# The up projection of two MLPs by seven block products in place of eight, in step with the down projection of the pair before

## The chip, the core and the metric

The kernel runs on one core of a Trainium2 chip. TensorE (PE) multiplies, VectorE (DVE) and ScalarE (ACT) prepare operands and take results out of PSUM, GpSimd (POOL) does little, and SyncE (SP) issues the loads from HBM. The metric is the device time of one execution in microseconds, the median of the runs.

## The reference

A hybrid decoder trunk of two layers over 256 tokens of width 2048, all in float32: a latent attention mixer (MLA), then a Mamba-2 mixer (SSM), each followed by a dense MLP with a squared relu. The MLPs are what the change is about:

```
for i in range(DEPTH):                       # DEPTH = 2
    h = rms_norm(x, mix_norm_g[i])
    mix = mla_mixer(h, ...) if i == 0 else ssm_mixer(h, ...)
    x = x + mix
    h = rms_norm(x, mlp_norm_g[i])
    x = x + squared_relu_mlp(h, mlp_w_in[i], mlp_w_out[i])

def squared_relu_mlp(h, w_in, w_out):        # (256, 2048), (2048, 8192), (8192, 2048)
    u = jax.nn.relu(h @ w_in)
    return (u * u) @ w_out
```

## The kernel before

**Three matmuls for one product.** TensorE is fed with a rounded float32 form. So each float32 operand is split into a high part h (the rounded value) and a low part lo (what is left), and a product is ah*wh + ah*wl + al*wh: the three `matmul` calls of `block` (lines 227 to 229). The stationary operand is a 128x128 tile of the activations, transposed (features on partitions, tokens in columns); the moving operand is a 128x512 tile of the weights. Results gather in a PSUM bank of 128 tokens by 512 columns.

**Weights.** `Flow` (line 59) holds a list of all weight pieces in the order of their use. A piece is 512 rows by 512 columns, 1 MB, laid out as 128 partitions by 4 k-tiles by 512 columns. `load` (line 70) issues its transfer on SP's queue into one of three `raw` buffers. `convert` (line 81) makes h and lo for half a piece at a time (two k-tiles, 1024 columns): a copy on ACT (line 101) into one of three `wh` buffers, then a subtraction on DVE (line 102) into one of three `wl` buffers. `piece` (line 106) hands out the halves; before it hands out one it has asked for loads three pieces on and conversions two halves on (`ahead`, (3, 2)).

**The MLP** (line 371). The hidden width of 8192 is cut into 16 blocks of 512 columns, taken four at a time, as a chunk. For each block the up projection runs over 16 k-tiles and two token tiles, 96 matmuls of 4 pieces, into two banks of the pool `acc` (4 banks). ACT takes each bank out with relu, scaled by the row's normalisation (line 384), and squares it (line 385). One step later four TensorE transposes (line 210) bring it into `yp` or `sm` (2 banks each), and `split_out` (lines 203, 204) makes h and lo of it in `k4` tiles. Behind the four blocks of a chunk comes their down projection: four column blocks of the output, each over the chunk's 16 k-tiles, 96 matmuls into two banks, which DVE adds to the residual x (line 307). In the last chunk `finalize` (line 275) also prepares the next layer's input, or the result is stored (line 398).

**What sets the order.** TensorE executes in the order in which the source issues. The other engines' and queues' orders are set when the kernel is built, by a scheduler that places an instruction where it expects its inputs and a free buffer; each engine then keeps to its order. `later(n, fn)` (line 153) puts small work, such as transposes, off by n further steps; `tick` (line 156) ends a step. Weight conversion, taking out of PSUM and residual additions share the queues of DVE and ACT.

The MLA and SSM stages use the same `block` and `Flow`. `boundary_begin` and `finalize` leave the next stage's input as four pairs of tiles (h and lo), each of 4 k-tiles by 256 tokens.

Of the kernel before, what the change touches and what calls it, by code (L numbers as in the profile page):

```python
# [20 lines left out]
F32 = mybir.dt.float32  # L21
F32R = mybir.dt.float32r
# [35 lines left out]

class Flow:


    def __init__(self, nc, pools, seq, ahead):
        self.nc, self.pools, self.seq, self.ahead = nc, pools, seq, ahead
        self.raw, self.loaded, self.used, self.done = {}, 0, 0, 0
        self.halves, self.split = [], {}
        for i, (_, _, nk, n) in enumerate(seq):
            step = nk if nk * n <= 1024 else nk // 2
            self.halves += [(i, k, step, n) for k in range(0, nk, step)]

    def load(self, upto, split=None, beside=None):  # L70
        while self.loaded < min(upto, len(self.seq)):
            _, src, nk, n = self.seq[self.loaded]
            t = self.pools["raw"].tile([P, 2048], F32, tag="raw", name=f"wr{self.loaded}")
            for o, z in split or ((0, nk * n),):
                self.nc.sync.dma_start(t[:, o:z], src[:, o:z])
                if split:
                    beside()
            self.raw[self.loaded] = t
            self.loaded += 1

    def convert(self, upto):
        while self.done < min(upto, len(self.halves)):
            j = self.done
            i, k, nk, n = self.halves[j]
            self.load(i + 1)
            raw = self.raw[i][:, k * n:(k + nk) * n]
            h = self.pools["wh"].tile([P, 1024], F32R, tag="wh", name=f"wh{j}")
            lo = self.pools["wl"].tile([P, 1024], F32R, tag="wl", name=f"wl{j}")
            if n == 64:
                for q, t in enumerate((h, lo)):  # L90
                    v = t.rearrange("p (k r n) -> p k r n", r=2, n=64)
                    w = raw.rearrange("p (k n) -> p k n", n=64)[:, 8 * q:8 * q + 8]
                    self.nc.scalar.activation(v[:, :, 0], w, AF.Copy)
                    self.nc.vector.tensor_tensor(v[:, :, 1], w, v[:, :, 0].bitcast(F32), ALU.subtract)
                self.split[j] = (h, lo)
                self.done += 1
                continue
            w = 512 if j == 0 else nk * n
            for o in range(0, nk * n, w):
                v = slice(o, o + w)  # L100
                self.last = self.nc.scalar.activation(h[:, v], raw[:, v], AF.Copy)  # L101
                self.nc.vector.tensor_tensor(lo[:, v], raw[:, v], h[:, v].bitcast(F32), ALU.subtract)  # L102
            self.split[j] = (h, lo)
            self.done += 1

    def piece(self, key):

        i = self.seq_at
        assert self.seq[i][0] == key, (self.seq[i][0], key)
        self.seq_at += 1  # L110
        while self.used < len(self.halves) and self.halves[self.used][0] == i:
            j = self.used
            self.load(i + self.ahead[0])
            self.convert(j + 1 + self.ahead[1])
            _, k, nk, n = self.halves[j]
            h, lo = self.split.pop(j)
            if n == 64:
                self.used += 1
                yield [t.rearrange("p (k n) -> p k n", n=P) for t in (h, lo)]
                return  # L120
            yield (k, nk, h[:, :nk * n].rearrange("p (k n) -> p k n", k=nk),
                   lo[:, :nk * n].rearrange("p (k n) -> p k n", k=nk))
            self.used += 1

    seq_at = 0


class Trunk:
    def __init__(self, tc, ctx, d, out):
# [9 lines left out]
        self.gb = pool("gb", 3)  # L139
        self.wp = {"raw": pool("raw", 3), "wh": pool("wh", 3), "wl": pool("wl", 3)}  # L140
# [65 lines left out]
    def transposes(self, src, h, lo, t, wide=True):  # L206

        b = self.bank(wide)
        for j in range(4):
            self.nc.tensor.transpose(b[:, j * P:(j + 1) * P], src[:, j * P:(j + 1) * P], self.ident)  # L210
        sl = slice(t * P, (t + 1) * P)
        self.split_out(h[:, :, sl], lo[:, :, sl], b.rearrange("p (k n) -> p k n", k=4))


    def block(self, keys, lhs, n=512, accs=None, first=True, last=True):
# [4 lines left out]
        for ik, key in enumerate(keys):  # L220
            for k, nk, wh, wl in self.flow.piece(key):
                for q in range(nk):
                    for t in range(2):
                        ah, al = lhs(kt, t)
                        st = first and kt == 0
                        en = last and ik == len(keys) - 1 and k + q == self.flow.seq[self.flow.seq_at - 1][2] - 1
# [7 lines left out]
    def narrow_block(self, key, tiles, then):  # L234
# [3 lines left out]
        (w,) = self.flow.piece(key)  # L238
# [26 lines left out]
    def boundary_begin(self, gain):  # L265
        self.nx = [None] * 4
        self.nx_ssq = self.stat(8)
        self.nx_gain = gain
# [6 lines left out]
    def finalize(self, nb, accs, wide=True):  # L275
        nc = self.nc
        g = self.gain_tile(self.nx_gain[nb])
        self.nx[nb] = (self.ktile(self.xtp), self.ktile(self.xtp))
        h, lo = self.nx[nb]
        for t in range(2):  # L280
            x = self.x[t][nb]
# [4 lines left out]
            self.later(0, lambda t=t, xg=xg: self.transposes(xg, h, lo, t, wide))  # L286
# [23 lines left out]
    def start(self, seq):  # L310
        nc, d = self.nc, self.d
        self.flow = Flow(nc, self.wp, seq, (3, 2))
# [16 lines left out]
        self.flow.load(1, ((0, 512), (512, 1024), (1024, 2048)), some_x)  # L329
        for j in range(1, 4):  # L330
            nc.sync.dma_start(raws[j], d["xT"][j])
            if j < 3:
                self.flow.load(j + 1)
# [18 lines left out]
        self.flow.load(4)  # L352
# [18 lines left out]
    def mlp(self, layer, gain):  # L371
        nc = self.nc
        xT = self.xT
        rs = self.rs
        for c in range(4):
            us = []
            for b in range(4):
                nb = c * 4 + b
                accs = self.block([("mi", layer, nb, q) for q in range(4)], self.from_tiles(xT))
                h, lo = self.ktile(self.k4), self.ktile(self.k4)  # L380
                us.append((h, lo))
                for t in range(2):
                    r = self.scratch()
                    nc.scalar.activation(r, accs[t], AF.Relu, scale=rs[t])  # L384
                    nc.scalar.activation(r, r, AF.Square)  # L385
                    self.later(0, lambda t=t, r=r, h=h, lo=lo: self.transposes(r, h, lo, t))
            if c == 3 and gain is not None:
                self.boundary_begin(gain)
            for nb in range(4):
                accs = self.block([("mo", layer, c, q, nb) for q in range(4)], self.from_tiles(us))  # L390
                if c < 3:
                    self.add_residual(nb, accs)
                elif gain is not None:
                    self.finalize(nb, accs)
                else:
                    for t in range(2):
                        x = self.x[t][nb]
                        nc.vector.tensor_tensor(x, accs[t], x, ALU.add)
# [733 lines left out]
```

## Time and profile before

| What | Value |
|---|---|
| Median of 3 runs | 2415.56 us (2414.2 to 2416.3) |
| The profiled execution | 2414.62 us, span 2412.8 us |
| Granted TensorE clock | 1.000 |
| Moved by DMA | 451.88 MB, mean 187 GB/s |
| First MLP, second MLP | 292 to 1003 us, 1697 to 2408 us |

The span is the time from the first to the last instruction in the trace. Busy times are those of the instructions as the trace draws them; matmuls are drawn longer than they are apart, since they overlap in the array. In the lines below a group is: source line, engine, operation, output tile <- input tiles, shapes, count, then busy time in us and mean ns of one, then how long the engine stood idle before them and which instruction ended that. In a timeline a row is: start in us, length in us, engine, line, operation.

### The profile page before, as it was taken

To read this page: it belongs to the slowest core of one execution; us is meant where nothing else is said; L and a number is where in the kernel's file an instruction comes from. 1 tells how busy PE (TensorE), PEld (TensorE's weight loads), DVE (VectorE), ACT (ScalarE), POOL (GpSimd) and SP (SyncE) were. 2 spreads that over 40 slices of the span, in tenths; PEclk is the share of its full clock that TensorE was granted. 3 is DMA by queue.
4 is the path that set the end of the run, shared out by engine and by line. 5 is a ranking of instruction groups with operands and counts; after the bars stand their busy time and mean duration, and the time that the engine had idled before them with its cause. 6 is when DMAs were issued, how large, how long until landed. Compare 5 with 4: busy or idle time off the path is not lost.

```text
span 2412.8 us, 28583 instructions
## 1 busy us (share of the span) xinstructions
PE 2389.9 (99%) x11136; PEld 1990.5 (82%) x11136; DVE 1427.8 (59%) x1911; ACT 1194.5 (50%) x1679; POOL 137.6 (6%) x152
## 2 busy tenths in 40 slices
PE   8999999999999999999999999999999999999999
PEld 6888888888888888888888888888888888888887
DVE  6676645544545445577789778666545454545444
ACT  6665554354354354455555455544543443443443
POOL 1340000000000000000022001110000000000000
PEclk9999999999999999999999999999999999999999
DMA  7333655555555555565465656555555555555554
GB/s 290 130 124 127 209 177 189 193 191 189 195 185 183 194 188 196 181 212 177 168 197 200 201 188 205 189 180 199 180 187 192 192 186 196 183 186 193 190 196 153
DMA packets 76680, 451.88 MB, mean 187 GB/s; under 512 B 8640, under 2 KB 17280, under 8 KB 25472
## 3 DMA queue, kind: packets, MB, share of 16 engines
q1 hardware_dynamic: 76464, 449.99, 54.4%
q8 instruction: 87, 1.43, 0.2%
q14 instruction: 49, 0.40, 0.0%
q10 hardware_dynamic: 80, 0.07, 0.0%
HBM read 447.86 MB, written 2.16 MB: 187 GB/s over the span
## 4 chain that ended last, share of the span: by engine, by line
PE 93%; DVE 3%; POOL 1%; ACT 1%; issue 1%; DMA 0%; SPq 0%; POOLq 0%; ACTq 0%; DVEq 0%
PE acc L227 29%; PE acc L229 29%; PE acc L228 29%; PE sm L210 1%; PE y L917 1%; DVE wl L102 1%; PE yp L210 1%; ACT wh L101 1%; POOL st L194 1%; DMA wr<-ain 0%; POOL ra L472 0%; ACT xt L632 0%; PE sm L759 0%; PE sm L881 0%; DVE kn L581 0%
## 5 line engine op out<-in xcount | busy, mean ns | idle before, releaser
L102 DVE TENSOR_TENSOR wl<-wr,wh 128x1024 fp32r<-128x1024 f32 (+2 forms) x817 | 1003.5, 1230 | 883.4 <-ACT wh L101 882.2
L101 ACT ACTIVATE wh<-wr 128x1024 fp32r<-128x1024 f32 (+2 forms) x817 | 862.9, 1057 | 1044.9 <-PE acc L229 1009.1
L227 PE MATMUL acc<-wh,xt 128*128 128x512 f32 x1728 | 682.0, 395 | 5.6 <-ACT wh L101 5.6
L228 PE MATMUL acc<-wl,xt 128*128 128x512 f32 x1728 | 674.0, 390 | 1.4 <-DVE wl L102 1.4
L229 PE MATMUL acc<-wh,xt 128*128 128x512 f32 x1728 | 674.4, 390 | 0.0
L227 PE MATMUL acc<-wh,k 128*128 128x512 f32 x1408 | 552.0, 392 | 0.0
L229 PE MATMUL acc<-wh,k 128*128 128x512 f32 x1408 | 548.4, 389 | 0.0
L228 PE MATMUL acc<-wl,k 128*128 128x512 f32 x1408 | 547.9, 389 | 0.0
L227 PEld LDWEIGHTS acc<-wh,xt 128*128 128x128 f32 x1728 | 325.2, 188 | 70.7 <-ACT wh L101 6.0
L228 PEld LDWEIGHTS acc<-wl,xt 128*128 128x128 f32 x1728 | 325.3, 188 | 68.2 <-DVE wl L102 3.0
L229 PEld LDWEIGHTS acc<-wh,xt 128*128 128x128 f32 x1728 | 324.9, 188 | 68.6
L229 PEld LDWEIGHTS acc<-wh,k 128*128 128x128 f32 x1408 | 264.2, 188 | 55.5
L228 PEld LDWEIGHTS acc<-wl,k 128*128 128x128 f32 x1408 | 264.5, 188 | 54.2 <-DVE wl L102 0.4
L227 PEld LDWEIGHTS acc<-wh,k 128*128 128x128 f32 x1408 | 264.4, 188 | 53.4
L194 POOL TENSOR_TENSOR st<-st,mhalf 128x4 f32<-128x4 f32 (+1 forms) x30 | 26.2, 872 | 1000.7 <-DVE st L193 985.6
L384 ACT ACTIVATE s<-acc,rs 128x512 f32<-128x512 f32 x64 | 43.6, 682 | 31.4 <-PE acc L229 31.4
L768 DVE SCALAR_TENSOR_TENSOR s<-sm,cst,s 128x255 f32<-128x255 f32 (+2 forms) x114 | 54.6, 479 | 2.8 <-ACT s L765 1.3
L905 DVE TENSOR_SCALAR mt<-cm,ncum 128x128 f32<-128x128 f32 x128 | 45.8, 398 | 7.6 <-PE y L917 7.6
L307 DVE TENSOR_TENSOR x<-acc,x 128x512 f32<-128x512 f32 x72 | 46.1, 683 | 0.0
L906 ACT ACTIVATE mt<-mt 128x256 f32<-128x256 f32 x64 | 26.2, 414 | 39.8 <-DVE mt L905 39.8
L908 DVE SCALAR_TENSOR_TENSOR mt<-mt,dt,cb 128x128 f32<-128x128 f32 x128 | 40.6, 360 | 1.6 <-ACT mt L906 1.5
L385 ACT ACTIVATE s<-s 128x512 f32<-128x512 f32 x64 | 40.2, 628 | 1.0
(240 smaller groups left out, 1320.7 us busy)
## 6 DMA issues: line engine op xcount, KB each, us to landing
wr<-mi SPq DMA_DIRECT2D x128, 1024.0 KB, 4.8
wr<-mo SPq DMA_DIRECT2D x128, 1024.0 KB, 4.8
wr<-si SPq DMA_DIRECT2D x80, 1024.0 KB, 4.9
wr<-so SPq DMA_DIRECT2D x32, 1024.0 KB, 4.9
wr<-wo SPq DMA_DIRECT2D x16, 1024.0 KB, 4.8
wr<-ukv SPq DMA_DIRECT2D x8, 1024.0 KB, 5.0
cm<-cumD SPq DMA_DIRECT2D x64, 128.0 KB, 3.2
wr<-ain SPq DMA_DIRECT2D x7, 1024.0 KB, 9.0
```

The lines of the kernel that those rows point to most:

```text
L101: self.last = self.nc.scalar.activation(h[:, v], raw[:, v], AF.Copy)
L102: self.nc.vector.tensor_tensor(lo[:, v], raw[:, v], h[:, v].bitcast(F32), ALU.subtract)
L194: nc.gpsimd.tensor_tensor(r, v, self.mhalf[:, :n], ALU.pow)
L210: self.nc.tensor.transpose(b[:, j * P:(j + 1) * P], src[:, j * P:(j + 1) * P], self.ident)
L227: nc.tensor.matmul(accs[t][:, :n], ah, wh[:, q, :], start=st, stop=False)
L228: nc.tensor.matmul(accs[t][:, :n], ah, wl[:, q, :], start=False, stop=False)
L229: nc.tensor.matmul(accs[t][:, :n], al, wh[:, q, :], start=False, stop=en)
L307: self.nc.vector.tensor_tensor(x, accs[t], x, ALU.add)
L384: nc.scalar.activation(r, accs[t], AF.Relu, scale=rs[t])
L768: nc.vector.scalar_tensor_tensor(o[:, m:256], s[:, 0:256 - m], wc(i), o[:, m:256], ALU.mult, ALU.add)
L905: nc.vector.tensor_scalar(half(t), cm[:, t * P:(t + 1) * P], ncum[:, t, h:h + 1], 0.0, ALU.add, ALU.min)
L908: nc.vector.scalar_tensor_tensor(half(t), half(t), dt[:, t, h:h + 1], cb[g][:, 256 * t:256 * t + P], ALU.mult, ALU.mult)
```

## The change

**Seven products.** The 16 hidden blocks become 8 pairs. Pair 0 is computed as before. In pairs 1 to 7 the input and the weights are cut in two each way. On the side of x, A11 and A12 are the two halves of the depth (1024 features, 8 k-tiles) for the first 128 tokens, A21 and A22 for the second. On the side of the weights, B11 and B12 are the upper halves of the pair's two column blocks, B21 and B22 the lower. The seven products, each over 8 k-tiles with 24 matmuls, have the names M1, N7, N5, N6, N4, M2 and N3 in the code:

```
M1 = A11 B11                      N7 = (A21-A11)(B12+B22)
N5 = (A21-A22)(B11+B12)           N6 = (A11-A21+A22)(B11+B12+B22)
N4 = A22 (B11+B12+B22+B21)        M2 = A12 B21
N3 = (A12-A11+A21-A22) B22
w = N6-M1;  c = N5+w
C11 = M1+M2;  C12 = N3+c;  C21 = N4-(w+N7);  C22 = N7+c
```

The combinations of x are made once per MLP (`combinations`), beside pair 0 and just behind it. Those of the weights are made for each quarter d of the half depth (two k-tiles, 512 KB): three DVE additions in place. The fourth addition, B21 onto the sum, is a GpSimd DMA that adds what it loads to what the tile holds. B21 and B22 are loaded once more for M2 and N3.

**The order.** A written pattern (PERIOD) of 44 steps interleaves a pair's 28 product steps (six matmuls on a converted tile) with 16 steps of the down projection ("o", twelve matmuls) of the pair before; the last column block of that one falls into the next period. In the first period the first four "o" are left out. The last column block of pair 6 and all of pair 7's down projection stand behind the last period. The down projection collects a pair (8 k-tiles) in a bank in place of four blocks (16 k-tiles), in the two `yp` banks; N7 collects in `sm`, the other products in `acc`.

**Loads and buffers.** Loads are 512 KB, the unit of conversion: six `raw` buffers of half the size in place of three, four `wh` and `wl` in place of three, loads 6 units ahead and conversions 3. B11 tiles have a pool of five (`r4`), the combinations of x one of their own (`mp`), both for the time of an MLP. Gain buffers (`gb`) go from three to two. Ahead of an MLP the boundary leaves its output by token tile and half depth (`by_tile`).

The diff, cut to its core:

```
 class Flow:
+    def halves(self, raw, n, step=None):
+        h = self.pools["wh"].tile([P, 1024], F32R, tag="wh", name=f"wh{self.done}")
+        lo = self.pools["wl"].tile([P, 1024], F32R, tag="wl", name=f"wl{self.done}")
+        for o in range(0, n, step or n):
+            v = slice(o, o + (step or n))
+            self.last = nc.scalar.activation(h[:, v], raw[:, v], AF.Copy)
+            nc.vector.tensor_tensor(lo[:, v], raw[:, v], h[:, v].bitcast(F32), ALU.subtract)
+        return h, lo
...
+    def next(self, key):
+        j, u = self.at, self.units[self.at]
+        self.load(j + 1 + self.ahead[0])
+        self.convert(j + 1 + self.ahead[1])
+        self.at += 1
+        return u, self.split.pop(j)
...
+def seven(layer, p, src, tokens):
+    def quarter(d, i, j):
+        return src[2 * i + d // 2, 2 * p + j][:, (d % 2) * 1024:(d % 2) * 1024 + 1024]
...
+        def make():
+            if name == "N7":
+                add(st["b22"], st["b12"], st["b22"])
+                return flow.halves(st["b22"].tile, 1024)
+            if name == "N5":
+                add(st["b12"], st["b11"], st["b12"])
+                return flow.halves(st["b12"].tile, 1024)
+            if name == "N6":
+                add(st["b11"], st["b11"], st["b22"])
+                hl = flow.halves(st["b11"].tile, 1024)
+                nc.gpsimd.dma_start(st["b11"].tile, quarter(d, 1, 0), accum_op=ALU.add)
+                return hl
+            return flow.halves(st[{"M1": "b11", "N4": "b11", "M2": "c21", "N3": "c22"}[name]].tile, 1024)
...
-        self.gb = pool("gb", 3)
-        self.wp = {"raw": pool("raw", 3), "wh": pool("wh", 3), "wl": pool("wl", 3)}
+        self.gb = pool("gb", 2)
+        self.wp = {"raw": pool("raw", 6), "wh": pool("wh", 4), "wl": pool("wl", 4)}
...
-        self.flow = Flow(nc, self.wp, seq, (3, 2))
+        self.flow = Flow(nc, self.wp, seq, (6, 3))
...
+        S, steps = self.combinations(mp, xa)
+        self.later(1, steps[0])
+        self.later(3, steps[1])
+        for j in range(2):
+            accs = self.block([("mi", layer, j, q) for q in range(4)], lhs_x)
...
+        steps[2]()
...
+        def down(pp, nb, o):
+            if o == 0:
+                out[nb] = [self.yp.tile([P, 512], F32, tag="yp", name=self.name("mo")) for _ in range(2)]
...
+            if o == 3:
+                self.add_residual(nb, out.pop(nb))
+        for p in range(1, 8):
...
+            def after(name, p=p, bank=bank, v=v):
+                if name == "M1":
+                    v["m1"] = self.scratch()
+                    nc.scalar.activation(v["m1"], bank["M1"], AF.Copy)
+                elif name == "N6":
+                    w, c, e = (self.scratch() for _ in range(3))
+                    sub(w, bank["N6"], v["m1"])
+                    plus(c, bank["N5"], w)
+                    plus(w, bank["N7"], w)
+                    plus(e, bank["N7"], c)
+                    v["c"] = c
+                    nc.scalar.activation(e, e, AF.Relu, scale=rs[1])
+                    v["w"] = w
+                    fn = hidden(e, p, 1, 1)
+                    self.later(3, lambda: fn(False))
...
+                    u, (h, lo) = self.flow.next(("st", layer, p, name, d))
+                    xh, xl = S[name]
+                    for q in range(2):
+                        k = 2 * d + q
+                        wh, wl = h[:, q * 512:(q + 1) * 512], lo[:, q * 512:(q + 1) * 512]
+                        nc.tensor.matmul(b, xh[:, k], wh, start=k == 0, stop=False)
+                        nc.tensor.matmul(b, xh[:, k], wl, start=False, stop=False)
+                        nc.tensor.matmul(b, xl[:, k], wh, start=False, stop=k == 7)
+                    if d == 3:
+                        after(name)
...
+PERIOD = """M1 N7 o N5 o N6 o  M1 o N7 N5 N4 o N6 o  M1 o N7 o N5 N6 N4 o
+M1 o N7 o N5 N6 o N4 o M2 o N4 N3 o M2 N3 o M2 N3 M2 N3""".split()
```

The folds of N4, M2 and N3 in `after` are one DVE operation each, then relu and square as for N6.

More of the change, by code (lines that the diff above doesn't have):

```diff
@@ L66, in __init__ @@
[L66 to L78, printed above, removed]
-            self.loaded += 1
@@ L81, in convert @@
-    def convert(self, upto):
[L82 to L103, printed above, removed]
-            self.done += 1
@@ L237, in narrow_block @@
         nc = self.nc
-        (w,) = self.flow.piece(key)
+        w = [t.rearrange("p (k n) -> p k n", n=P) for t in self.flow.next(key)[1]]
         acc = self.bank(False)
@@ L371, in mlp @@
     def mlp(self, layer, gain):
-        nc = self.nc
[L373 to L381, printed above, removed]
-                for t in range(2):
[L383 to L394, printed above, removed]
-                else:
-                    for t in range(2):
-                        x = self.x[t][nb]
-                        nc.vector.tensor_tensor(x, accs[t], x, ALU.add)
-                        nc.sync.dma_start(self.out[t * P:(t + 1) * P, nb * 512:(nb + 1) * 512], x)
```

297 lines of the change are left out of this document (256 added, 41 removed).

## The prediction

> **What bounds the kernel now.** I read the page's busy table and chain first, to see which engine carries the span; then busy time by stage; then the groups by line with shapes kept apart; then the timelines of PE, DVE and ACT inside the first MLP; then the DMA view.
>
> ```profile
> PE 2389.9 (99%) x11136; PEld 1990.5 (82%) x11136; DVE 1427.8 (59%) x1911; ACT 1194.5 (50%) x1679; POOL 137.6 (6%) x152
> PE 93%; DVE 3%; POOL 1%; ACT 1%; issue 1%; DMA 0%; SPq 0%; POOLq 0%; ACTq 0%; DVEq 0%
> ...
> 0.00:292.00 292.00, 275.58 (x1404) 234.81 (x1405) 192.89 (x419) 174.22 (x444) 58.46 (x87) 1.00 0.49 174
> 292.00:1003.00 711.00, 711.00 (x3219) 590.43 (x3218) 359.78 (x338) 332.27 (x375) 1.78 (x3) 1.00 0.55 190
> 1003.00:1697.00 694.00, 691.95 (x3311) 575.16 (x3310) 521.85 (x832) 363.58 (x504) 76.27 (x59) 1.00 0.57 191
> 1697.00:2408.00 711.00, 711.00 (x3207) 590.12 (x3205) 352.25 (x325) 324.48 (x357) 1.07 (x3) 1.00 0.55 187
> ```
>
> The columns of the last four are stretch, length, then busy time of PE, PEld, DVE, ACT, POOL, the granted clock, DMA share and GB/s. The two MLPs are the second and fourth stretch: 711 us each, PE busy throughout at clock 1.00, DVE at 51%, POOL idle. A busy PE is not by itself a full one, so I look at the spacing.
>
> ```profile
> 500.03 0.39 PE L229 MATMUL acc<-wh,xt 128*128 128x512 f32 x1
> ...
> 502.75 0.39 PE L229 MATMUL acc<-wh,xt 128*128 128x512 f32 x1
> ...
> 1332.29 0.87 PE sm L210 x8
> ```
>
> Twelve matmuls start in 2.72 us, one per 0.2267 us, although each is drawn 0.39 us long; eight transposes take 0.87 us. One MLP has 3072 matmuls and 128 transposes: 696.4 + 13.9 = 710.3 us against the 711 seen. So each MLP is a solid row of matmuls, and its time is their number.
>
> **What is removed.** A column pair in the up projection takes 192 matmuls (2 blocks x 16 k-tiles x 2 token tiles x 3), seven products of half depth take 7 x 24 = 168. That is 24 x 0.2267 = 5.44 us less in each pair; seven pairs in each of two MLPs: 14 x 5.44 = **76.2 us**. I call the work of one pass of the new order (one pair up, another pair down, 44 steps) a period: PE needs 360 x 0.2267 + 16 transposes (1.74) = 83.3 us, against 88.8 for the same work now. A product step is six matmuls, 1.36 us; a down step twelve, 2.72 us.
>
> **What DVE gets.**
>
> ```profile
> L102 DVE TENSOR_TENSOR wl<-wr,wh 128x1024 fp32r<-128x1024 f32 x799 | 987.3, 1237 | 878.9 <-ACT wh L101 877.6
> L101 ACT ACTIVATE wh<-wr 128x1024 fp32r<-128x1024 f32 x799 | 848.0, 1062 | 1031.6 <-PE acc L229 996.8 <-issue 24.6 <-DVE wl L102 6.5
> ...
> L307 DVE TENSOR_TENSOR x<-acc,x 128x512 f32<-128x512 f32 x72 | 46.1, 683 | 0.0
> ...
> L384 ACT ACTIVATE s<-acc,rs 128x512 f32<-128x512 f32 x64 | 43.6, 682 | 31.4 <-PE acc L229 31.4
> ...
> L385 ACT ACTIVATE s<-s 128x512 f32<-128x512 f32 x64 | 40.2, 628 | 1.0
> ...
> L204 DVE TENSOR_TENSOR k<-sm,k 128x512 fp32r<-128x512 f32 x52 | 34.8, 683 | 0.0
> ...
> L203 ACT ACTIVATE k<-sm 128x512 fp32r<-128x512 f32 x52 | 30.0, 592 | 0.5 <-PE sm L660 0.3
> ```
>
> Now one weight tile of 1024 columns costs one copy on ACT (L101) and one subtraction on DVE (L102) and feeds 12 matmuls. In the change a tile of a combined weight feeds only six, and is summed first on DVE. Per period: 28 product tiles and 16 down tiles, 44 subtractions, and 12 sums (three in each of four quarters, same shape and operands as L102, so its price): 56 operations of the 1024 kind. Of the 512 kind, 7 that fold the products from PSUM, 8 residual additions (now 4, since a bank collected four column blocks and will collect two) and 4 subtractions after transposes: 19. By mean durations 56 x 1.237 + 19 x 0.683 = **82.3 us of DVE in 83.3 us of PE**; today the same work takes 32 x 1.237 + 8 x 0.683 = 45. But a duration isn't the spacing:
>
> ```profile
> 389.60 1.23 DVE L102 TENSOR_TENSOR wl<-wr,wh 128x1024 fp32r<-128x1024 f32 x1 [1.50 <-ACT wh L101]
> 390.74 0.68 DVE L204 TENSOR_TENSOR k<-yp,k 128x512 fp32r<-128x512 f32 x1
> 391.34 0.68 DVE L204 TENSOR_TENSOR k<-sm,k 128x512 fp32r<-128x512 f32 x1
> ...
> 404.10 1.23 DVE L102 TENSOR_TENSOR wl<-wr,wh 128x1024 fp32r<-128x1024 f32 x1 [1.50 <-ACT wh L101]
> 405.24 1.28 DVE L307 TENSOR_TENSOR x<-acc,x 128x512 f32<-128x512 f32 x2
> ```
>
> Where DVE has the next operation ready, it starts 1.14 us after a long one and 0.60 after a short one. So 56 x 1.14 + 19 x 0.60 = 75.2 us, 90% of the period. I take this, since DVE will mostly have a queue, and keep 82.3 as the other end. The Trainium skill's page "VectorE: DVE Perf Modes" (The DRAIN you can't avoid) says that the next operation doesn't start until the pipe has emptied, and that only operations that aren't held start earlier; read strictly, the whole duration counts, and the sum would be that of the second rival, 2390. The rows above disagree with the strict reading by 0.09 us for each operation.
>
> ACT needs 44 x 1.062, a copy and four squared relus (5 x 0.682 + 4 x 0.628) and four copies of 0.592: 55 us, two thirds, so it is no bound. It matters that DVE doesn't stand still for the 1.06 us of ACT between a sum and its subtraction. The orders of ACT and DVE are fixed at build time, not as written:
>
> ```profile
> 383.64 0.67 ACT L384 ACTIVATE s<-acc,rs 128x512 f32<-128x512 f32 x1
> 384.21 1.05 ACT L101 ACTIVATE wh<-wr 128x1024 fp32r<-128x1024 f32 x1
> 385.16 0.62 ACT L385 ACTIVATE s<-s 128x512 f32<-128x512 f32 x1
> ```
>
> A conversion has slipped between a relu and its square, adjacent in the source; sums, which need no wh buffer, can fill DVE's gaps alike.
>
> **Where PE will wait.** With four wh/wl buffers a tile may be converted from the end of the step four before it: three product steps (4.08 us), less copy and subtraction (2.30), leave DVE 1.8 us of arrears. Going along the order with spacings:
> - The six steps M2 N3 M2 N3 M1 N7 across the period's edge, with one residual pair and two folds in them: DVE 7 x 1.14 + 4 x 0.60 = 10.4, PE 6 x 1.36 + 0.43 = 8.6. Arrears 1.8, just covered: 0 to 1.8.
> - The twelfth and thirteenth down step, with one N4 (1.36 us) between them: both banks must be emptied in that time, which takes 1.28 (L307 x2) plus up to a conversion: 0 to 1.1.
> - M2's fold, relu, square (2.0 us and up to 2.2 of queues) before its transposes 4.08 us later: 0 to 0.2. Those transposes share one bank with N3's, a down step (2.72) apart; emptying takes 1.3 to 3.5: 0 to 0.8.
>
> Together 0 to 3.9 us per period; I take 1.4, nearer to the low end because 90% leaves DVE 8 us per period to catch up in: 14 x 1.4 = **19.6**. The first period of each MLP lacks four down steps at its start: eight product steps, 10.9 us of PE, against 13 long operations and the last three of the combinations of x, less five done ahead: 11 x 1.237 = 13.6, so 2.7 late; with two of the five not ahead 5.2, with the sums done under the classical pair 0. I take **3 us** each, 6 in all. The other combinations of x (9 long DVE operations) lie under the classical first pair (43.5 us of PE, about 22 of DVE); without that cover they'd cost 11.1 each time.
>
> **DMA.**
>
> ```profile
> q1 hardware_dynamic: 76464, 449.99, 54.4%
> ...
> wr<-mi SPq DMA_DIRECT2D x128, 1024.0 KB, 4.8
> ...
> wr<-ainr SPq DMA_DIRECT2D x1, 512.0 KB, 8.1
> wr<-sidt SPq DMA_DIRECT2D x1, 512.0 KB, 3.4
> ...
> L75 SPq DMA_DIRECT2D wr<-mo x128: 327/328/340, 365.5 to 2386.3; - x128
> ```
>
> Lower-half quarters are fetched twice, so a period moves 40 x 0.524 = 21 MB: 252 GB/s. 450 MB kept the engines busy for 54.4% of 2412.8 us, so full is about 343 GB/s, and 252 is 73%. At the period's edge eight loads fall into 10.9 us (385 GB/s), 1.3 us late if nothing were ahead, but loads run six steps ahead: nothing. SP issues 36 loads at 0.328 us, 12 of 83 us; a load that waits for a buffer holds the later ones in that queue.
>
> The one new kind of transfer is GpSimd's adding one: it waits until ACT and DVE have read N6's tile, lands B21 on it, and N4's copy on ACT waits for it, with all later copies queued behind, and PE behind those. POOL itself has nothing else (1.78 us of 711). From the start of N6 to where N4 must be converted (2.3 us ahead of its step) there are 8.5, 12.6, 16.6 and 9.8 us in the four quarters. The trace has no adding transfer; 1 MB landed in 4.8 us in the MLP, 512 KB in 3.4 on a quiet queue and 8.1 in the opening rush. All are under 8.5, and with the queues at 73% the quiet rows are nearest: I take 4 to 6 us, so no wait. The Trainium skill, "DMA: Bandwidth & Descriptors" (Anatomy of one DMA), gives a GpSimd-issued DMA 2.0 us and bytes / 436 GB/s, an estimate of 3.2 us here; by it too the sum is unchanged, but no run here shows it.
>
> **Outside the MLPs** tiles are converted three ahead in place of two, and gain buffers fall from 3 to 2. PE stands still for 16.4 us in the first stretch and 2.1 in the third; a deeper lead can win some of that, or push short operations back: -8 to +8, I take 0.
>
> **Sum**, on the profiled execution (2414.6 us: span 2412.8 and 1.8 around it; the runs' median is 0.9 above it): 2414.6 - 76.2 + 19.6 + 6 = 2364.0, as a median **2365 us**.
>
> **Rivals.**
> - *All is hidden*: no stall, 2339. For it: 10% of DVE is free and steps are interleaved. Against: places above with no reserve. Chance 0.2.
> - *DVE becomes the bound*: whole durations count, 82.3, and it stands still 5% of the time behind a copy or PE: 86.6 per period, 3.3 over PE: 2414.6 - 76.2 + 46 + 6 = 2390; up to no change at 88.8. For it: the 82.3. Against: the spacing rows. Chance 0.2, a fifth of that within the same. The strict reading of the Trainium skill's page above is this case.
> - *The adding transfer is late*, the one that ends slower: at landing L a period loses (L - 8.5) + (L - 9.8), above 12.6 also that quarter. At 13 us: 4.5 + 3.2 + 0.4 = 8.1, and 14 x 8.1 + 6 - 76.2 gives 2458. With nothing else lost it decides at L = 11.9 (5.4 us per period). For it: each byte is also read back from SBUF and the kind is unknown; against: 3.4 to 8.1 for this size. Chance 0.15, of which 0.01 is within the same.
> - The forecast, 2345 to 2385, has 0.45. That the matmuls are not fewer cannot be: their number is in the source.
>
> **Numbers.** Faster by over 0.2% (4.8 us, about what a measurement here can tell): 0.2 + 0.45 + 0.16 = 0.81; same 0.05; slower 0.14. The range goes from 2332 (all hidden, with 7 of the 8 us gained outside) to 2410 (DVE as the bound, close to no change) and leaves out the slow transfer and little else; the forecast's own is 2345 to 2385.
>
> **What would show it.** 11,136 - 336 = 10,800 on PE; spacing still 0.2267; DVE busy near 640 of each MLP's 686 us (7 x (40 x 1.237 + 7 x 0.683) = 380, 128 down tiles 158, 64 additions 44, 32 after transposes 22, the first pair with the combinations 28 x 1.237 = 35); 450 + 14 x 8 x 0.524 = 509 MB in loads; 56 adding transfers landing in under 8 us; PE's idle time ended by DVE subtractions, some 1.4 us per period, at the period's edge and after the twelfth down step. I'd be wrong if PE waits chiefly on ACT copies released by a GpSimd DMA, or if DVE's spacing in the MLP is 1.24.

## The result and the profile after

The change made the kernel slower: 2438.34 us median of 4 runs (2436.93 to 2442.57) against 2415.14 (2414.2 to 2416.3), a ratio of 1.0099, 95% interval 1.0081 to 1.0116. The profiled execution took 2442.57 us, span 2440.7. The forecast of 2365 had the wrong sign, and its range ended 28 us below.

The page of the kernel after: busy time, queues (packets, MB, share of the engines' time), the adding transfers (KB, median us to landing).

```profile
PE 2354.8 (96%) x10800; PEld 1930.3 (79%) x10800; DVE 1919.2 (79%) x2433; ACT 1388.3 (57%) x1869; POOL 187.2 (8%) x208
...
q1 hardware_dynamic: 143136, 479.38, 61.5%
q0 software_dynamic: 8064, 29.36, 7.4%
...
wr<-mi POOLq DMA_DIRECT2D x56, 512.0 KB, 8.1
```

The 336 fewer operations on PE are there, and so are the bytes. PE is busy for 35 us less than before, and the span is 28 us longer: the gain was turned into idle time. Where, the busy time by stage tells (the stage borders are PE's first matmul of each stage; columns as in the prediction).

```profile
0.00:299.20 299.20, 277.95 (x1405) 237.31 (x1405) 196.90 (x421) 174.86 (x444) 59.17 (x86) 0.98 0.54 172
299.20:1024.20 725.00, 695.07 (x3066) 560.38 (x3065) 605.07 (x599) 430.78 (x472) 26.51 (x32) 0.99 0.76 228
1024.20:1713.70 689.50, 687.42 (x3292) 571.80 (x3291) 521.35 (x831) 361.30 (x502) 76.23 (x59) 1.00 0.64 191
1713.70:2440.70 727.00, 694.35 (x3043) 560.81 (x3041) 595.92 (x585) 421.35 (x452) 25.27 (x31) 0.99 0.74 223
```

By the same borders the kernel before has 292.2, 714.3, 690.0 and 716.3. So the first stage lost 7.0 us, each MLP 10.7, the SSM stage nothing: 28 together. The forecast had taken 25.3 off each MLP (689.0 and 691.0); both came out 36.0 above it. PE now has 30 and 33 us without work in the two MLPs, and the clock is 0.99 where it was 1.00.

The waits inside the first MLP's seven periods (us in total, times, the longest):

```profile
DVE wraw L175 <- DMA wraw<-mi: 32.8, 17, 3.9
...
PE sm L293 <- DVE k L283: 13.6, 6, 2.3
...
ACT wh L102 <- DMA wr<-mi: 6.7, 5, 2.7
...
PE mo L558 <- DVE x L399: 5.4, 7, 0.8
PE st L617 <- DVE wl L103: 4.9, 10, 0.6
PE mo L559 <- DVE wl L103: 4.5, 7, 0.7
```

The largest wait of PE comes at the edge between two periods: transposes (L293) into `sm` wait for a subtraction (L283) that reads that bank. One of the six, on DVE, on ACT and on PE (start, length, what; in brackets idle time before it and what ended it):

```profile
514.38 0.68 DVE L568 TENSOR_TENSOR s<-st,s 128x512 f32<-128x512 f32 x1
514.98 1.21 DVE L175 TENSOR_TENSOR wraw<-wr,wraw 128x1024 f32<-128x1024 f32 x1
516.23 1.23 DVE L175 TENSOR_TENSOR wr<-wr,wraw 128x1024 f32<-128x1024 f32 x1
517.47 2.36 DVE L103 TENSOR_TENSOR wl<-wraw,wh 128x1024 fp32r<-128x1024 f32 x2
519.75 0.68 DVE L283 TENSOR_TENSOR k<-sm,k 128x512 fp32r<-128x512 f32 x1
```

```profile
515.10 0.72 ACT L598 ACTIVATE s<-s,rs 128x512 f32<-128x512 f32 x1 [0.34 <-DVE s L568]
515.85 0.63 ACT L517 ACTIVATE s<-s 128x512 f32<-128x512 f32 x1
516.39 1.99 ACT L102 ACTIVATE wh<-wraw 128x1024 fp32r<-128x1024 f32 x2
518.29 0.57 ACT L282 ACTIVATE k<-sm 128x512 fp32r<-128x512 f32 x1
```

```profile
514.80 0.66 PE L293 MATMUL sm<-cst,s 128*128 128x128 f32 x4
...
517.82 0.39 PE L560 MATMUL mo<-wh,k 128*128 128x512 f32 x1
520.49 0.66 PE L293 MATMUL sm<-cst,s 128*128 128x128 f32 x4 [2.28 <-DVE k L283]
...
521.97 0.63 PE L616 MATMUL st<-wh,sN 128*128 128x512 f32 x1
522.40 0.63 PE L617 MATMUL st<-wl,sN 128*128 128x512 f32 x1
...
524.86 0.39 PE L559 MATMUL mo<-wl,k 128*128 128x512 f32 x1
```

M2's transposes run on time at 514.80. ACT copies their bank only behind N3's relu and square (L598, L517) and two conversions, at 518.29, and is done 3.6 us after the transposes; DVE subtracts only behind two sums and two conversions, at 519.75, 0.9 us later still. All twelve such waits of the two MLPs show the same two lengths. N3's transposes, wanted behind the down step that ends at 518.2, go into the same bank and stand until 520.49. Then something is seen that the forecast had no term for: until 524.86 the matmuls start 0.43 us apart in place of 0.23. That is half the clock, for ten matmuls. It happened after eight of the twelve such waits; the last section shows what parts the eight from the four.

Adding up over the seven periods of each MLP by how much the next start on PE exceeds 0.2267 us (0.109 for a transpose), from every PE row of the trace:

| us per seven periods | first MLP | second MLP |
|---|---|---|
| Matmuls and transposes alone | 583.5 | 583.5 |
| N3's transposes wait for the bank | 14.6 | 14.6 |
| Matmuls spaced wider (half clock, and 0.1 on the first after a wait) | 11.2 | 13.7 |
| Waits for weight subtractions (L617, L559) | 12.1 | 9.4 |
| Down step waits for a residual addition (L558) | 6.5 | 6.5 |
| Rest | 5.6 | 5.5 |
| Measured | 633.5 | 633.2 |

The eight half-clock stretches hold 12.5 us of the third row.

### The profile page after: what moved, and what is told of

The parts are those of the page before. It is cut to its first block, busy times and chain, and to the rows that moved or that the text cites. A ratio compares the mean times of both kernels' runs of the same rounds, so it can differ in the third digit from the quotient of the medians.

```text
span 2440.7 us, 30283 instructions
## 1 busy us (share of the span) xinstructions
PE 2354.8 (96%) x10800; PEld 1930.3 (79%) x10800; DVE 1919.2 (79%) x2433; ACT 1388.3 (57%) x1869; POOL 187.2 (8%) x208
## 3 DMA queue, kind: packets, MB, share of 16 engines
q1 hardware_dynamic: 143136, 479.38, 61.5%
q0 software_dynamic: 8064, 29.36, 7.4%
## 4 chain that ended last, share of the span: by engine, by line
PE 56%; DVE 19%; issue 10%; DMA 9%; ACT 3%; POOL 2%; SPq 0%; DVEq 0%; ACTq 0%; POOLq 0%
PE acc L309 11%; PE acc L311 11%; PE acc L310 11%; DVE wl L103 11%; DMA wraw<-mi 8%; PE mo L559 4%; PE mo L558 4%; PE mo L560 4%; DVE wraw L175 2%; PE st L618 2%; PE st L617 2%; PE st L616 2%; ACT wh L102 2%; DVE x L399 2%; DVE s L568 1%
## 5 line engine op out<-in xcount | busy, mean ns | idle before, releaser
L102 ACT ACTIVATE wh<-wraw 128x1024 fp32r<-128x1024 f32 (+2 forms) x817 | 860.5, 1055 | 740.5 <-PE acc L311 301.9
L103 DVE TENSOR_TENSOR wl<-wraw,wh 128x1024 fp32r<-128x1024 f32 (+2 forms) x817 | 995.7, 1226 | 307.6 <-ACT wh L102 296.2
L558 PE MATMUL mo<-wh,k 128*128 128x512 f32 x896 | 355.3, 397 | 10.7 <-DVE x L399 10.7
L559 PE MATMUL mo<-wl,k 128*128 128x512 f32 x896 | 352.5, 393 | 7.8 <-DVE wl L103 7.7
L560 PE MATMUL mo<-wh,k 128*128 128x512 f32 x896 | 350.4, 391 | 0.0
L309 PE MATMUL acc<-wh,xt 128*128 128x512 f32 x832 | 331.9, 399 | 6.3 <-ACT wh L102 6.2
L310 PE MATMUL acc<-wl,xt 128*128 128x512 f32 x832 | 325.5, 391 | 0.8 <-DVE wl L103 0.8
L311 PE MATMUL acc<-wh,xt 128*128 128x512 f32 x832 | 325.8, 392 | 0.0
L103 DVE TENSOR_TENSOR wl<-wr,wh 128x1024 fp32r<-128x1024 f32 x168 | 204.6, 1219 | 46.1 <-ACT wh L102 44.1
L558 PEld LDWEIGHTS mo<-wh,k 128*128 128x128 f32 x896 | 169.9, 190 | 56.8 <-DVE x L399 16.8
L559 PEld LDWEIGHTS mo<-wl,k 128*128 128x128 f32 x896 | 169.5, 189 | 49.5 <-DVE wl L103 15.5
L309 PE MATMUL acc<-wh,k 128*128 128x512 f32 x512 | 202.7, 396 | 0.0
L311 PE MATMUL acc<-wh,k 128*128 128x512 f32 x512 | 199.7, 390 | 0.0
L310 PE MATMUL acc<-wl,k 128*128 128x512 f32 x512 | 199.3, 389 | 0.0
L560 PEld LDWEIGHTS mo<-wh,k 128*128 128x128 f32 x896 | 169.1, 189 | 35.6
L617 PE MATMUL st<-wl,xt 128*128 128x512 f32 x448 | 176.4, 394 | 6.8 <-DVE wl L103 6.7
L616 PE MATMUL st<-wh,xt 128*128 128x512 f32 x448 | 177.1, 395 | 0.0
L618 PE MATMUL st<-wh,xt 128*128 128x512 f32 x448 | 174.9, 390 | 0.0
```

The lines of the kernel that those rows point to most:

```text
L102: self.last = nc.scalar.activation(h[:, v], raw[:, v], AF.Copy)
L309: nc.tensor.matmul(accs[t][:, :n], ah, wh[:, q, :], start=st, stop=False)
L310: nc.tensor.matmul(accs[t][:, :n], ah, wl[:, q, :], start=False, stop=False)
L311: nc.tensor.matmul(accs[t][:, :n], al, wh[:, q, :], start=False, stop=en)
L558: nc.tensor.matmul(b, ah, wh, start=kt == 0, stop=False)
L559: nc.tensor.matmul(b, ah, wl, start=False, stop=False)
```

## The theories and the experiments

**Theory 1.** The loss in the MLPs is the shared bank at the period's edge, with the half clock and the waits for subtractions that follow from it; DVE as a whole has time enough. **Rivals:** DVE's load as such sets the pace (theory 2); loads wait for raw buffers, SP's queue stands long on them (theory 3); the adding transfer is late (theory 4); the smaller units alone cost something in every stage. With each edit the scheduler may order DVE and ACT anew; where that bears on a reading, the order was taken from the traces.

**1. `n3_later`: the transposes of N3 two steps later.** This is the `later` behind the fold of N3; nothing else changes in the source.

```
-                    self.later(3, lambda: fn(False))
+                    self.later(5, lambda: fn(False))
```

> N3's transposes are put off by two more steps. Theory 1 (a few waits at fixed places of the order): the 2.3 us wait on the one free sm bank goes, and with it the slow matmuls behind it; 14 x about 3.8 us, to about 2385 us, clock back towards 1.000. Theory 2 (DVE is the bound): the arrears only come out somewhere else, at most 15 us are won, 2423 or more. Theory 3 (loads come late for want of raw buffers): as theory 2.

Measured: 2392.62 us, ratio to before 0.9899 (0.9884 to 0.9914). The seven periods took 603.9 us in place of 633.5, the wait for the bank is gone, the clock is 0.999. One constant moves the time by 46 us, from a loss to a gain.

**2. `no_adding`: without the GpSimd transfer that adds B21**, so N4 lacks that term.

```
-                nc.gpsimd.dma_start(st["b11"].tile, quarter(d, 1, 0), accum_op=ALU.add)
```

> The adding GpSimd transfer is left out (N4 is computed without B21). Theory 4 (that transfer is late and holds ACT): most of the loss goes, 2380 or less. Theories 1 to 3: the sm wait, the yp wait and the waits on subtractions stay, 2425 to 2440.

Measured: 2425.1 us, 1.0038 (1.0023 to 1.0054): 13 us less than with it, and still slower than before. The wait for the bank stays at 13.6 us in six times; what falls, added up as in the table, is PE's waits for subtractions (from 21.5 us in both MLPs to 11.5) and the half clock (five stretches in the MLPs in place of eight, 7.8 us in place of 12.5). PE, DVE and ACT execute in the same order in both traces, so the first fall is the transfer's; the second is a matter of where the same waits happened to lie (last section). So the transfer does cost something, which I had put at nothing, but a part of the 13 us is chance, and it is not what turned the sign. Whether it still costs 13 us once the bank is free was not tried.

**3. `raw_7`: one raw buffer more**, paid for with two scratch tiles.

```
-        self.s2 = pool("s2", 8)
+        self.s2 = pool("s2", 6)
-        self.wp = {"raw": pool("raw", 6), "wh": pool("wh", 4), "wl": pool("wl", 4)}
+        self.wp = {"raw": pool("raw", 7), "wh": pool("wh", 4), "wl": pool("wl", 4)}
```

> One more raw buffer (seven), paid for with two scratch buffers (six). Theory 3 (want of raw buffers): SP's wait for a free buffer and DVE's waits on loads (61 us) fall by a third or more and the MLPs get 10 to 25 us shorter each. Theory 1: DVE waits less on loads, but PE's waits stay within 3 us per MLP, unless scratch becomes short. Theory 2: no change in the MLPs.

Measured: 2437.35 us, 1.0087 (1.0067 to 1.0107), the same as the change. The waits from 400 to 960 us show why:

```profile
DVE wraw L175 <- DMA wraw<-mi: 25.3, 14, 3.1
...
PE sm L293 <- DVE k L283: 13.6, 6, 2.3
```

With one buffer more SP stands on the release of raw buffers as long as without (441.7 us against 430.9 in the same window): its queue runs ahead and is held there anyway. DVE still waits for loads at times, but PE's wait is the same six times 2.3. PE and ACT execute in the same order as in the change, DVE does not (204 of its 2433 places differ). As far as one buffer can test it, the theory of the raw buffers falls.

**4. `units_only`: the MLP of before in the new frame**: 512 KB units, six raw buffers, four `wh` and `wl`, two gain buffers, loads 6 and conversions 3 ahead; `combinations`, `seven` and the period are not used, and the MLP runs by chunks as before. Seen from the kernel before, the core of what is left of the diff is this (`Flow` stays as in the change):

```
-        self.gb = pool("gb", 3)
-        self.wp = {"raw": pool("raw", 3), "wh": pool("wh", 3), "wl": pool("wl", 3)}
+        self.gb = pool("gb", 2)
+        self.wp = {"raw": pool("raw", 6), "wh": pool("wh", 4), "wl": pool("wl", 4)}
...
-        self.flow = Flow(nc, self.wp, seq, (3, 2))
+        self.flow = Flow(nc, self.wp, seq, (6, 3))
```

> The MLPs as before, but with the change's 512 KB loads, six raw and four wh and wl buffers, loads 6 and conversions 3 units ahead, and two gain buffers. If the 7 us that the first stage lost come from these and not from the MLP: 2421 to 2423, with the wait of the fold in the first stage at 7 to 8 us and both MLPs at 711. If they come from the MLP's new pools and layout: 2415.

Measured: 2420.72 us, 1.0019 (1.001 to 1.0029). Its first two stages:

```profile
0.00:297.40 297.40, 277.31 (x1404) 236.74 (x1405) 194.72 (x420) 175.09 (x445) 60.32 (x87) 0.99 0.54 173
297.40:1011.70 714.30, 714.30 (x3233) 593.17 (x3232) 361.49 (x339) 332.81 (x376) 1.77 (x3) 1.00 0.63 190
```

The MLP takes what it took before, 714.3. All of the loss, 5.2 us, lies in the first stage. So the smaller units cost nothing in the MLP, and most of the first stage's 7.0 us is theirs. The other 1.8 us are a stretch of half clock from 81.0 us that this run, with the same short waits ahead of it, doesn't have. In the trace of the change the 5.2 us are one place. PE, then DVE of the change, then DVE of the kernel before:

```profile
48.34 1.12 PE L332 MATMUL sm<-cst,s 128*128 128x64 f32 x4 [7.59 <-DVE s L327]
```

```profile
39.16 1.23 DVE L103 TENSOR_TENSOR wl<-wraw,wh 128x1024 fp32r<-128x1024 f32 x1 [1.53 <-DMA wraw<-ain]
...
47.87 0.41 DVE L327 COPY s<-sm 128x256 f32<-128x256 f32 x1
```

```profile
42.78 0.42 DVE L245 COPY s<-sm 128x256 f32<-128x256 f32 x1
```

The same copy, which releases a fold on PE, comes 5.1 us later: 16 conversions stand ahead of it in DVE's order in place of 12, and one of them waits 1.53 us for a load, with the short operations behind it. PE's wait of 7.59 us (1.5 before) leaves half clock behind it as well, until 53.7.

**5. `n3_period`: the period's end rewritten**, on top of run 1, to part the twelfth and thirteenth down step.

```
-M1 o N7 o N5 N6 o N4 o M2 o N4 N3 o M2 N3 o M2 N3 M2 N3""".split()
+M1 o N7 o N5 N6 o N4 M2 o N3 o N4 M2 o N3 o M2 N3 M2 N3""".split()
```

> On top of N3's later transposes the pattern puts two product steps, not one, between the twelfth and thirteenth down step. Theory 1: the 0.93 us wait for the two yp banks goes in each period, 13 us, to about 2380. Theory 2 (DVE is the bound): the wait comes out elsewhere, 2388 to 2393.

Measured: 2429.07 us, 1.005 (1.0033 to 1.0067), 36 us worse than run 1. The waits of its first MLP:

```profile
PEld sm L293 <- ACT s L517: 21.3, 14, 2.4
...
PE sm L293 <- ACT s L517: 14.9, 9, 2.0
```

The wait of L558 that it was made to remove is gone, as meant. But N6's transposes, three steps after N6, now come after fewer matmuls, ahead of the square (L517) that they read: up to 2.0 us each time, and the clock is down to 0.990 again. The edit moved the stall to the next fixed distance.

**6. `n3_no_sums`: run 1 without the three DVE sums of each quarter**, so that the products use plain weights.

```
-        add = lambda out, a, b: nc.vector.tensor_tensor(out.tile, a.tile, b.tile, ALU.add)
+        add = lambda out, a, b: None
```

> N3's transposes later, and the three DVE sums of each quarter are left out (the products use the plain tiles), 13.7 us less DVE work per period. Theory 1: the waits on subtractions go, the yp wait stays; the periods of an MLP fall from 604 to about 596 us each, 2376. Theory 2: all waits go, the periods fall to 585 to 588 each, 2356.

Measured: 2382.39 us, 0.9859 (0.9839 to 0.9879), 10 us below run 1. The first MLP's seven periods:

```profile
343.20:943.40 600.20, 590.53 (x2637) 482.75 (x2636) 451.45 (x442) 378.35 (x405) 24.87 (x29) 1.00 0.81 242
```

DVE is freed of 78 us in these periods (451 busy, 530 in run 1), and they get 3.7 us shorter. DVE's load is not the bound.

**7 and 8. `n3_period_fold` and `before_fold`: the first stage's fold two steps later**, on top of run 5, and in the kernel before.

```
-        self.later(1, fold)
+        self.later(3, fold)
```

> As n3_period, and the fold of the narrow projection at the start of the kernel is put off by two more steps, so that TensorE doesn't wait 7.6 us there. If the first stage's loss is this one wait: 5 to 7 us under n3_period, about 2374. If the work behind is late as well: no gain.

> The kernel before, with the same later fold. TensorE waits 1.7 us there before the change: 2413 to 2415, so that the later fold is a repair of the changed kernel rather than a gain by itself.

Measured: 2417.05 us, 1.0003 (0.9994 to 1.0013), against 2429.07 without it on the same chip; and 2416.51, 1.0 (0.9991 to 1.001). The change gets its first stage back (289.75 us in place of 297.7); in the kernel before, where PE had waited 1.5 us at that place, the edit brings nothing. So the fold is a loss of the change's units, not an old one found by chance.

**9. `n3_bank`: N3's transposes at their old place, into another bank.** This is the sharper test of the theory: all 10,800 operations on PE stay in their order, and the bank's reuse goes. DVE's order, made anew, differs at 264 of its 2433 places, ACT's at 24 of 1869.

```
+        if wide == "acc":
+            return self.acc_tile()
...
-                    self.later(3, lambda: fn(False))
+                    self.later(3, lambda: fn("acc"))
```

> N3's transposes stay where the change has them, but write to a free bank of the acc pool in place of the shared sm bank. If the wait is the bank's (emptied late because DVE's fixed order puts sums and conversions ahead of it): it goes, about 2385 to 2395, as with the later transposes. If N3's fold, relu and square are late as well: a wait of over 1 us per period released by ACT's square stays, 2410 or more.

Measured: 2380.95 us, 0.986 (0.9846 to 0.9875). Its two MLPs, then the waits in the first:

```profile
297.70:991.60 693.90, 685.47 (x3065) 558.74 (x3064) 602.02 (x599) 428.71 (x472) 26.53 (x32) 1.00 0.78 238
...
1681.20:2379.00 697.80, 683.23 (x3043) 556.26 (x3040) 592.70 (x585) 419.14 (x452) 25.29 (x31) 1.00 0.76 232
```

```profile
PE mo L560 <- DVE x L401: 5.4, 7, 0.8
...
PE st L619 <- DVE wl L103: 0.9, 2, 0.6
PE mo L561 <- DVE wl L103: 0.6, 2, 0.4
```

And M2's bank at one of the periods' edges, on PE, ACT and DVE:

```profile
508.80 0.66 PE L295 MATMUL sm<-cst,s 128*128 128x128 f32 x4
...
512.29 0.57 ACT L284 ACTIVATE k<-sm 128x512 fp32r<-128x512 f32 x1
...
513.75 0.68 DVE L285 TENSOR_TENSOR k<-sm,k 128x512 fp32r<-128x512 f32 x1
```

The bank is emptied as late as before, 5.2 us after its transposes, but nothing waits for it. The profiled execution is 61.7 us shorter than that of the change (2380.85 against 2442.57; the medians differ by 57.4). In the two times seven periods (602.4 and 604.1 us) the bank waits had been 29.2 us; with them went the half clock (12.5 us, no such stretch is left) and 14.7 of the 21.5 us of waits for subtractions. The half clock hung on the bank waits, since it stood right behind them. That the subtractions did, too, is only argued: while PE stands, it releases no `wh` and `wl`, so conversions behind it start late. DVE's new order can have a share in it, and run 2 brought these waits down with the bank waits left in place. What was not touched stands: the residual addition, 6.5 us in each MLP.

**10. `n3_fold`: run 1 with the later fold.** Against run 1:

```
-        self.later(1, fold)
+        self.later(3, fold)
```

> N3's transposes later, the change's own pattern, and the fold of the first stage two steps later. From 2393 less the 7 to 8 us that the fold won in the first stage: 2385. If the gain there depends on the build's order of DVE: 2390 or more.

Measured: 2380.92 us, 0.9857 (0.9843 to 0.9872), first stage 290.2. Against run 1, on another chip, 11.7 us less.

**11. `period_spread`: run 7 with N6's transposes, too, two steps later.** The edit is that of run 1, now behind the fold of N6:

```
-                    self.later(3, lambda: fn(False))
+                    self.later(5, lambda: fn(False))
```

> The pattern with two product steps between the twelfth and thirteenth down step and the later fold (2417), with N6's transposes put off by two more steps as well, since these came 1.4 us too early for their relu and square. Theory 1: that wait (15 us per MLP) goes with the slow matmuls behind it, and the yp wait stays away: 2370 to 2380. Theory 2: 2385 to 2417.

Measured: 2376.77 us (2375.84 to 2378.74), 0.9842 (0.9825 to 0.9858), the fastest of all. Three of its stages:

```profile
0.00:289.40 289.40, 276.24 (x1404) 236.33 (x1405) 196.76 (x421) 174.88 (x444) 59.00 (x86) 0.99 0.55 178
289.40:986.10 696.70, 686.09 (x3066) 560.23 (x3065) 601.58 (x599) 427.95 (x472) 26.54 (x32) 1.00 0.78 237
...
1675.60:2373.80 698.20, 684.09 (x3043) 557.54 (x3041) 592.45 (x585) 417.96 (x452) 25.29 (x31) 1.00 0.76 232
```

The new order that lost 36 us in run 5 is a gain, 4 us against run 10, once the transposes behind it are moved with it. The largest wait of PE that is left in its periods is for subtractions (6.5 us in the first MLP).

**12. `n3_pool`: run 1 with the sums on GpSimd**, which is nearly idle.

```
-        add = lambda out, a, b: nc.vector.tensor_tensor(out.tile, a.tile, b.tile, ALU.add)
+        add = lambda out, a, b: nc.gpsimd.tensor_tensor(out.tile, a.tile, b.tile, ALU.add)
```

> N3's transposes later, and the three sums of each quarter made on GpSimd in place of DVE. If GpSimd and DVE share the SBUF ports without loss: as without the sums, 2382, unless the longer sums themselves come late. If each holds the other up (DVE's two-input operations against a GpSimd operation that reads SBUF): DVE's operations grow beyond 1.24 us and the time rises over 2393.

Measured: 2493.35 us, 1.0321 (1.0301 to 1.0342), 101 us above run 1. Groups by line of this run, then one of the change:

```profile
L103 DVE TENSOR_TENSOR wl<-wraw,wh 128x1024 fp32r<-128x1024 f32 x799 | 1165.1, 1470 | 308.3 <-ACT wh L102 300.0 <-DMA wraw<-ain 1.5
...
L103 DVE TENSOR_TENSOR wl<-wr,wh 128x1024 fp32r<-128x1024 f32 x168 | 305.6, 1820 | 53.5 <-ACT wh L102 51.9
...
L175 POOL TENSOR_TENSOR wraw<-wr,wraw 128x1024 f32<-128x1024 f32 x56 | 182.7, 3262 | 4.4
```

```profile
L103 DVE TENSOR_TENSOR wl<-wr,wh 128x1024 fp32r<-128x1024 f32 x168 | 204.6, 1219 | 46.1 <-ACT wh L102 44.1
```

A sum takes 3.26 us on GpSimd in place of 1.22, and DVE's subtractions get longer, 1219 to 1820 ns in the mean of that group. What was taken off DVE came back as slower work on DVE: it is busy for 2017.7 us, against 1913.3 in run 1, with 168 operations fewer. How much of the 101 us is this, and how much the sums' own lateness, was not parted.

## Why the prediction was wrong, point by point

**What held.** The saving: 10,800 operations on PE, matmuls still 0.2267 us apart. DVE's work: its durations in the first MLP add up to 639.5 us, where 640 were forecast (605 busy, since overlaps count once). The bytes: 479.38 + 29.36 = 508.7 MB of 509. DVE's spacing of 1.14 us (two conversions in 2.36, and 517.47 to 519.75 above). The places: the stalls are at the period's edge and behind the twelfth down step, and the latter cost 0.93 us each, in the range of 0 to 1.1. The start of the first period: in the first MLP three waits of 1.17, 0.68 and 0.56 us in its first 36 us, 2.4 where 3 were taken (four in the second, 3.6).

**The step that failed** is this one: "Those transposes share one bank with N3's, a down step (2.72) apart; emptying takes 1.3 to 3.5: 0 to 0.8." Emptying took 5.2 us: from 514.80 plus four transposes of 0.109 to 520.49. I had allowed one long operation ahead of the copy and of the subtraction, as in a queue that is seldom full. At this place ACT had N3's relu and square and two conversions ahead of the copy, and DVE two sums and two conversions ahead of the subtraction, because the six steps across the edge all bring such work. Of the 5.2 us, 3.6 passed until ACT's copy was done, 0.9 in DVE's queue behind that, and 0.7 in the subtraction itself. I priced the edge and the bank as two points, as if the bank's readers had their queues for themselves. With the 1.8 us of DVE's arrears from the first point added, the emptying would have had 5.3 as its upper end and the wait 2.6; that this comes so near to the measured 5.2 and 2.3 is luck, since ACT's queue made the larger part.

**The term that was missing** is what such a wait sets off. The forecast added stalls, each once, and had no term for the clock. Here twelve stalls of 2.4 us brought half clock (12.5 us in all) and, as far as run 9 shows it, waits for subtractions (14.7). By run 9 the bank cost 60.3 us in the two MLPs, of the 78.6 between the forecast, 2364.0, and the profiled execution. My upper bound for all places of a period was 3.9 us, and 7.1 were lost.

**Outside the MLPs** I took 0 of -8 to +8; it was +7.0, of which 5.2 come from one wait (runs 4, 7 and 8). The size lies within the bounds, and the forecast names the reason ("push short operations back"), but not the copy that was then pushed back 5.1 us.

**The adding transfer**, taken at no cost: it landed in 5.7 to 9.8 us, median 8.1, not in 4 to 6, and leaving it out wins 13 us, some of it by chance (run 2). This rival had the right sign, not the mechanism: at 8.1 us it stays below its own point of decision, 11.9, and ACT stood on landings in these tiles, plain and adding together, for 14.1 us in ten times over the whole run (6.7 in the waits above). The nearest row was that of the opening rush (8.1), which I held for an end; the rows of quiet loads, which I took, were no guide.

**The rival of DVE as the bound** is refuted (run 6: 78 us less work on DVE, 3.7 us less time). The chance that the fault lay in order, not in load, stood nowhere: none of the rivals was a wait at one place that repeats, though the working listed these places.

With the bank freed (run 9) the two MLPs are 4.9 and 6.8 us above the forecast, and 2381 lies in the forecast's own range of 2345 to 2385: the mechanism of the gain was right, its placing in the schedule was not checked against what stands ahead in the queues.

## What to carry to other kernels

Where a row of matmuls without gaps is made shorter by giving the other engines more work, price each reuse of a PSUM bank by all that is queued ahead of its readers at that place, arrears included, not by the readers' own durations. A fixed distance such as "three steps later" is a promise about time; when the steps get shorter or are reordered, each such distance has to be set anew, and it costs one constant. Count a wait of about 2 us on TensorE at more than itself, since half clock often came with it here, and perhaps late operands.

## What the runs showed of the hardware

**Half clock after short waits.** After eight of the twelve bank waits of 2.28 us, six to ten matmuls ran 0.43 us apart, 1.3 to 1.7 us lost each time. None of the waits of 0.76 us for a residual addition (L558) was followed by one; with the bank free there was no such stretch in the periods. The granted clock in the traces tells when: it is 0.5 for stretches of 3.41 us, sometimes several in a row, which start whole multiples of 3.41 us apart, as on a fixed grid. Here are two neighbouring stretches of the change with the wait from 518.2 to 520.5, then two with the one from 608.9 to 611.3 (columns as in the prediction, the clock is the third number from the end):

```profile
517.90:521.32 3.41, 1.13 (x8) 0.79 (x7) 3.41 (x4) 2.98 (x5) 0.00 (x0) 1.00 0.75 222
521.32:524.73 3.42, 3.42 (x10) 2.63 (x9) 3.27 (x5) 1.52 (x2) 0.87 (x1) 0.50 0.98 282
...
606.65:610.07 3.41, 2.44 (x11) 1.67 (x9) 3.36 (x4) 3.38 (x6) 0.00 (x0) 1.00 0.59 169
610.07:613.48 3.41, 2.14 (x12) 1.83 (x13) 3.41 (x5) 2.20 (x4) 0.77 (x1) 1.00 0.80 274
```

The first wait lies within one stretch; with 0.2267 us for each matmul and 0.109 for each transpose PE fills 24% of it, and the next is at half clock. The second wait is cut by the border at 610.07, PE fills 66% and 57%, and the clock stays. Counted so for the stretches at full clock in both MLPs, in all eleven traces with the seven products, half clock came next in all 48 cases where PE filled 38% of a stretch or less, and in none of the 4440 where it filled 39% or more. So here about 2.1 us of idle time within one stretch decided, and it was chance that eight of the twelve waits lay so. Two short waits can add up: at the end of run 11's first MLP 1.19 and 0.64 us fell into one stretch, and nine matmuls ran at half clock behind them. The Trainium skill, "TensorE: Matmul & The Clock Gate" (Part 1: The HAM clock gate), has the clock fall to half after at least one idle window of about 3.4 us, in windows that run freely, and gives 426.7 ns for a 512-column matmul at half clock. The 0.43 us and the 3.41 us agree; the window did not have to be idle as a whole here.

**GpSimd beside DVE.** Run 12's rows above: DVE's subtraction from 1219 to 1820 ns while GpSimd adds in SBUF. The Trainium skill, "SBUF — State Buffer" (SBUF: two separate sides), says that a DVE operation with two SBUF inputs and a GpSimd operation exclude each other for a whole instruction through a shared port. The rows fit that, but the traces don't show the port itself.

**An adding transfer** of 512 KB landed in 8.1 us (median), a plain one of the same size and source in 4.7 to 5.0. Whether the adding or the issue from GpSimd makes the difference, no run here parts.
